# A searched table of leads sets every instruction's place in the scheduler's order; squares on ScalarE; the tail in two halves

## The chip, the core and the metric

The kernel runs on one core of a Trainium2 chip. A core has five engines that run their own instruction streams side by side: TensorE (PE in the profile; PEld is its weight load), VectorE (DVE), ScalarE (ACT), GpSimd (POOL) and SyncE (SP, which here issues the transfers). The metric is the device time of one execution in microseconds (us).

## The reference

A two-layer encoder over 512 tokens of width 1024, in float32. Cut to what is computed:

```
for l in range(2):
    z = rms_norm(x, g_mix) @ w_in            # q, k, v, recurrent input, gate
    o = rms_norm(diff_attention(rope(q), rope(k), v))      # 4 heads, two softmaxes each
    c = centred_dwconv(xb)
    r = rms_norm((rg_lru(c, forward) + rg_lru(c, backward)) * gelu(gb))
    x = x + concat(o, r) @ w_out
    x = x + cross_attention(rms_norm(x), rms_norm(mem))    # 4 heads, 256 tokens
    x = x + square(relu(rms_norm(x) @ w1)) @ w2            # 4096 wide
return rms_norm(x, g_final)
```

## The kernel before, in words

Activations lie feature-major: x is eight tiles `c_x0` to `c_x7` of 128 features by 512 tokens. A float32 product is made from two reduced-precision parts: each operand is split into a high part (a copy on ScalarE) and a low part (a subtraction on VectorE), and TensorE adds three products (high by high, high by low, low by high). A weight tile of 128 by 1024 is loaded by SP into `wraw`, and split into `whi` (ScalarE) and `wlo` (VectorE); there are three buffers of each. PSUM has three banks `mm` and five `at`.

**Stages.** Per layer: the mixer (input projection, differential attention, conv, recurrence with sigmoid gates, GeLU, and as filler between the heads the keys and values of the memory), the output projection and cross-attention, and the MLP. The MLP works in four blocks of 1024 hidden features. In a block `mlp_pair` (L1180) makes two hidden tiles: product, times the broadcast rstd `rb` on VectorE, and relu squared, also on VectorE (`t = max(t, 0) * t`); `left_pair` builds sums and differences of them and splits these. `seven` (L1000) multiplies a pair of weight tiles with seven products of half-size (Strassen-like) instead of eight, and adds each product to x on VectorE; `right_pair` prepares the weights in `wraw`, `pt`, `whi`, `wlo`.

**The tail.** After the last block the squares of all eight x tiles are added on VectorE into one tile (`nrm.add`), TensorE sums them over the features by a product with a column of ones (each of these float32 products shows as two records), VectorE scales and GpSimd takes the power -1/2, TensorE spreads the result over the partitions by transposes against `c_ident` (tile `at`), ScalarE copies it to `rb`. VectorE multiplies six tiles (already scaled by g_final on ScalarE), GpSimd two, and SP writes the eight tiles of 256 KB.

**What sets the order.** The kernel records every operation in a plan (`Plan.record`, L226) with a key: the TensorE time recorded so far, less a lead given by the code (`plan.ahead`: 12 us for splits, 65 us for loads, 3 us for attention). `Plan.schedule` (L272) then plays a list scheduler: engine by engine it places the operation with the smallest key that can start first by a table of assumed durations; an operation that needs another activation table gets 25 us added to its key (`SWITCH`). The outcome is a fixed order for each engine's in-order stream, emitted from L414; so nearly every row of the profile shows L414, and rows are told apart by tile names. Each engine waits on semaphores for the operands and the buffers of its next instruction, and whatever stands behind a waiting instruction waits too.

Of the kernel before, what the change touches and what calls it, by code (L numbers as in the profile page):

```python
# [11 lines left out]
F32 = mybir.dt.float32  # L12
# [31 lines left out]
ORDER = ["XYPp1Rr2B3bNK", "XY1Pp2Rr3BbNK"]  # L44
FILL = [[8.6, 7.6, 8.6, 7.6, 10.8, 9.7, 11.9, 6.5, 11.9, 7.6, 8.6, 10.8, 7.6, 5.4, 5.4, 7.6],
        [10.8, 7.6, 8.6, 7.6, 8.6, 10.8, 6.5, 10.8, 10.8, 10.8, 7.6, 7.6, 9.7, 3.2, 1.1, 6.5]]
LAG = 2
POOL_OUT = (0, 1)
ATT_AHEAD = 3
SPLIT_AHEAD = 12.0  # L50
LOAD_AHEAD = 65.0


PC = {}
# [96 lines left out]
class Plan:  # L151
# [7 lines left out]
    TABLE = 1.283  # L159
    SWITCH = 25.0  # L160
    WAIT = 2.5
    SETS = {"Exp": ("exp",), "Tanh": ("exp", "sig", "gelu"), "Sigmoid": ("sig",), "Sqrt": ("sqrt",),
            "Gelu_apprx_tanh": ("gelu",), "Sin": ("sin",)}

# [30 lines left out]
    def cost(self, eng, m, a, k):  # L195
        out = a[0] if a else k["out"]
        n = 1
        for d in out.shape[1:]:
            n *= d
        if eng == "pe":  # L200
            if m == "transpose":
                return 0.109
            f32 = a[1].root.dtype == F32
            if n < 64:
                return 0.224
            return n * 0.00176 if f32 else max(0.114, n * 0.000456)
        if m == "dma_start":
            return 0.06
        if eng == "act":
            t = 0.093 + n * 0.000833  # L210
            t += 0.093 * sum(isinstance(k.get(x), _View) for x in ("scale", "bias", "accum_out"))
            return t
        if eng == "dve":
            if m == "tensor_reduce":
                n = 512
            if m == "tensor_scalar_mul":
                return 0.066 + n * 0.0007
            ap = m == "scalar_tensor_tensor" and isinstance(a[2], _View)
            return 0.067 + n * 0.00105 + 0.06 * ap
        if eng == "pool" and n <= 4:  # L220
            return 1.0
        if eng == "pool":
            return 0.1 + n * (0.0022 if m != "memset" else 0.001)
        return 0.06

    def record(self, eng, m, a, k):  # L226
# [18 lines left out]
        if m == "dma_start":  # L245
            v = out[0] if out else k["in_"]
            op.bytes = 4
            for d in v.shape:
                op.bytes *= d
        if m == "activation":  # L250
            op.table = self.SETS.get(str(a[2]).split(".")[-1])
        for v in allv:
# [18 lines left out]

    def schedule(self):  # L272
        ops = self.ops
        for op in ops:
            op.preds.discard(op)
            op.behind -= op.preds | {op}
            op.npred = len(op.preds) + len(op.behind)
            for p in op.preds:
                p.succ[op] = True
            for p in op.behind:  # L280
                p.succ[op] = False
# [34 lines left out]
        def look(e):  # L316
            best, smin, tries = [], 1e18, 0
            for key, idx in cand[e]:
                op = ops[idx]
                st = max(free_at[e], op.ready)  # L320
                ok = True
                need = {}
                for r in op.new:
                    if r.tag in slots:
                        need[r.tag] = need.get(r.tag, 0) + 1
                for tag, n in need.items():
                    fr = sorted(slots[tag])[:n]
                    st = max(st, fr[-1])
                    w, h = waiting[tag], head[tag]
                    while h < len(w) and w[h] in placed:  # L330
                        h += 1
                    head[tag] = h
                    if st >= 1e17:
                        ok = False
                    elif w[h] != idx and n + sum(i > w[h] for i in alive[tag]) > spare[tag]:
                        ok = False
                tries += 1
                if ok:
                    if op.table and table not in op.table:
                        key += self.SWITCH  # L340
                        st += self.WAIT if st > free_at[e] else 0.0
                    best.append((st, key, idx))
                    smin = min(smin, st)
                if tries >= 60 and best:
                    break
            if not best:
                return None
            lim = smin + self.LOOK
            return min(((k, i, s) for s, k, i in best if s <= lim))

        dirty = set(self.engines)
        while left:
# [8 lines left out]
            _, idx, st = choice[e]  # L361
            op = ops[idx]
            cand[e].remove((op.key, idx))
            dur = op.dur
# [52 lines left out]
def trunk(tc, ctx, xT, memT, pos, W, par, outT):  # L417
# [18 lines left out]
    def T():  # L436
        return plan.tile("b", [P, S], F32)
# [24 lines left out]
    def raw_weight(l, t, ahead=None):  # L462
# [8 lines left out]
                SP.dma_start(out=raw, in_=W[l * NT + t])  # L471
        return raw

    def weight(l, t):
        raw = pre.pop(t, None) if l == 0 else None
        first = raw is not None
        if raw is None:
# [43 lines left out]
    def pc(l, name, i):  # L521
        o = l * NPL + PC[name] + i
        return prm[:, o:o + 1]

    ident = C([P, P], F32, "ident")
    G.memset(ident, 0.0)
# [470 lines left out]
        out[3] = [(dh[:, i * P:(i + 1) * P], dh[:, 512 + i * P:512 + (i + 1) * P]) for i in range(4)]  # L997
        return out

    def seven(l, ta, tb, left, ca, cb, order=range(4)):  # L1000

        w = right_pair(l, ta, tb)
        X, Y, Z = MM(), AT(), AT()
# [15 lines left out]
        add(ca, LO, X, ALU.add)  # L1019
        prod(2, Z, True)  # L1020
        add(ca, LO, Z, ALU.add)
        prod(6, X, False)
        add(cb, LO, X, ALU.subtract)
        prod(5, Y, True)
# [155 lines left out]
    def mlp_pair(l, bk, p, xs, rb):  # L1180

        ts = []
        for i in (2 * p, 2 * p + 1):
            pm = MM()
            gemm_fm(l, T_W1 + 8 * bk + i, xs, pm)
            t = T()
            V.tensor_tensor(t, pm, rb, op=ALU.mult)
            V.scalar_tensor_tensor(t, t, 0.0, t, op0=ALU.max, op1=ALU.mult)
            ts.append(t)
        return left_pair(*ts)  # L1190

# [21 lines left out]
    for l in range(DEPTH):  # L1213
# [64 lines left out]
        def finish(hd, h):  # L1278
# [3 lines left out]
                cat[h] = hd.out()  # L1282
            later(1, out)

        for u in range(16):
            h, qc = divmod(u, 4)
            if qc == 0:
# [50 lines left out]
        for bk in range(4):  # L1338
# [2 lines left out]
                nrm = Norm()  # L1341
                xs = [None] * KD
            for m in range(0, 8, 2):
                seven(l, T_W2 + 8 * bk + m, T_W2 + 8 * bk + m + 1, hid, m, m + 1)
                for c in (m, m + 1) if bk == 3 else ():
                    if l + 1 < DEPTH:
                        xs[c] = prep_x(l + 1, "g_mix", c, nrm)
                    else:
                        nrm.add(x[c])
                        xs[c] = T()  # L1350
                        A.activation(xs[c], x[c], AF.Copy, scale=prm[:, P_FINAL + c:P_FINAL + c + 1])
# [4 lines left out]
    rt = nrm.rstd(D, 4)  # L1356
    bp = AT()
    bcast(rt, 4, bp)
    rb = plan.tile("rb", [P, S], F32)
    A.activation(rb, bp, AF.Copy)  # L1360
    for c in POOL_OUT + tuple(c for c in range(KD) if c not in POOL_OUT):
        o = T()
        if c in POOL_OUT:
            G.tensor_tensor(o, xs[c], rb, op=ALU.mult)
        else:
            V.tensor_tensor(o, xs[c], bp, op=ALU.mult)
        SP.dma_start(out=outT[c * P:(c + 1) * P, :], in_=o)

    order = plan.schedule()
    plan.emit(tc, order)  # L1370
# [73 lines left out]
```

## Time and profile before

| | us |
|---|---|
| median of 3 runs | 1506.97 (1505.68 to 1511.34) |
| the profiled execution's own time | 1508.43 |
| its span, first to last instruction | 1506.6 |
| TensorE busy in it | 1446.8 (96%) |
| VectorE busy | 1159.3 (77%) |
| ScalarE busy | 731.7 (49%) |
| GpSimd busy | 26.5 (2%) |
| mean granted TensorE clock | 0.984 of full |

The span is what the trace shows; the profiled execution took 1.8 us more than it, and 1.5 us more than the median. A stage is read from a table of windows: the length of a window less TensorE's busy time is what TensorE waited, and the granted clock tells whether it ran at 2.4 GHz (1.00) or 1.2 GHz (0.50). The mixers lie at 30 to 200 us and 760 to 950 us, the MLPs at 408 to 760 us and 1145 to 1491 us.

### The profile page before, as it was taken

The page shows a single profiled execution, that of the slowest core. Times are in us where ns is not written, and L with a number is a line of the kernel's source. Part 1 is how long each engine was busy: PE and PEld are TensorE (multiplying, and loading weights), DVE is VectorE, ACT ScalarE, POOL GpSimd, SP SyncE. Part 2 cuts the span into 40 slices and gives each one's busy share as a digit, 9 for nine tenths or more (in the row PEclk, how much of TensorE's full clock was granted, in tenths as well). Part 3 has the DMA queues.
Part 4 walks back from the last instruction along what each step waited for, and adds up shares of the span by engine and source line. Part 5 has one row for each costly group of instructions (what it writes and reads, how often), then busy time and mean ns, then how long its engine had stood idle before and what let it go on. Part 6 is the DMA issues. An engine that isn't in the chain of part 4 may idle for free.

```text
span 1506.6 us, 20763 instructions
## 1 busy us (share of the span) xinstructions
PE 1446.8 (96%) x8038; PEld 1239.1 (82%) x8038; DVE 1159.3 (77%) x1959; ACT 731.7 (49%) x1105; POOL 26.5 (2%) x46
## 2 busy tenths in 40 slices
PE   8978999999999999999999989999999999999996
PEld 6756888888888989898887768888888898988985
DVE  7888886555679797887958799855556887969695
ACT  6587765334434343433534887643443433434343
POOL 1000000000000000000000000000000000000000
PEclk9988999999999999999999999999999999999998
DMA  5332442321222222222224444432122223232321
GB/s 198 112 101 71 144 153 92 112 70 43 99 97 93 104 99 98 98 96 101 85 103 121 112 106 149 137 112 83 59 70 84 99 99 112 82 104 89 118 84 58
DMA packets 47666, 152.43 MB, mean 101 GB/s; under 512 B 6096, under 2 KB 6224, under 8 KB 47568
## 3 DMA queue, kind: packets, MB, share of 16 engines
q1 hardware_dynamic: 47424, 150.85, 30.2%
q8 instruction: 63, 1.03, 0.3%
q14 instruction: 35, 0.29, 0.1%
q10 hardware_dynamic: 144, 0.26, 0.1%
HBM read 136.41 MB, written 2.10 MB: 92 GB/s over the span
## 4 chain that ended last, share of the span: by engine, by line
PE 80%; DVE 11%; ACT 4%; issue 2%; DMA 1%; SPq 1%; POOL 0%; DVEq 0%; ACTq 0%; POOLq 0%
PE mm L414 63%; PE at L414 18%; DVE b L414 6%; DVE wlo L414 3%; ACT b L414 3%; DVE pt L414 1%; ACT L414 1%; SPq L414 1%; DMA b<-b 1%; DVE s L414 1%; ACT whi L414 0%; POOL s L414 0%; DVE c_x L414 0%; DMA wraw<-in_memT 0%; DMA c_x<-in_xT 0%
## 5 line engine op out<-in xcount | busy, mean ns | idle before, releaser
L414 PE MATMUL mm<-b,whi 128*128 128x512 f32 (+1 forms) x3648 | 985.5, 358 | 11.7 <-ACT b L414 5.0
L414 PEld LDWEIGHTS mm<-b,whi 128*128 128x128 f32 x3648 | 638.5, 189 | 119.7 <-ACT b L414 6.3
L414 PE MATMUL mm<-b,wlo 128*128 128x512 f32 (+1 forms) x1824 | 650.1, 356 | 10.2 <-DVE wlo L414 10.2
L414 ACT ACTIVATE whi<-wraw 128x1024 fp32r<-128x1024 f32 (+1 forms) x223 | 233.4, 1048 | 357.4 <-issue 155.2
L414 PEld LDWEIGHTS mm<-b,wlo 128*128 128x128 f32 x1824 | 344.5, 189 | 67.4 <-DVE wlo L414 12.6
L414 DVE TENSOR_TENSOR wlo<-wraw,whi 128x1024 fp32r<-128x1024 f32 (+1 forms) x223 | 268.9, 1206 | 40.9 <-ACT whi L414 40.4
L414 DVE TENSOR_TENSOR b<-b,b 128x512 fp32r<-128x512 f32 (+2 forms) x390 | 224.7, 593 | 16.0 <-ACT b L414 14.4
L414 ACT ACTIVATE b<-b 128x256 fp32r<-128x256 f32 (+2 forms) x224 | 130.3, 596 | 150.2 <-DVE b L414 146.7
L414 DVE TENSOR_TENSOR c_x<-c_x,mm 128x256 f32<-128x256 f32 (+1 forms) x160 | 73.7, 471 | 77.8 <-PE mm L414 76.4
L414 ACT ACTIVATE whi<-pt 128x1024 fp32r<-128x1024 f32 x64 | 67.9, 1061 | 101.8 <-PE mm L414 75.7
L414 PE MATMUL at<-b,whi 128*128 128x256 f32 x512 | 92.0, 278 | 0.0
L414 DVE TENSOR_TENSOR b<-mm,rb 128x512 f32<-128x512 f32 x72 | 49.4, 687 | 53.5 <-PE mm L414 53.4
L414 DVE TENSOR_TENSOR wlo<-pt,whi 128x1024 fp32r<-128x1024 f32 x64 | 78.1, 1220 | 0.6 <-ACT whi L414 0.3
L414 ACT ACTIVATE b<-at,s 128x512 f32<-128x512 f32 (+2 forms) x100 | 61.0, 617 | 34.8 <-DVE s L414 34.1
L414 PEld LDWEIGHTS at<-b,whi 128*128 128x128 f32 x512 | 77.7, 188 | 0.0
L414 PE MATMUL at<-b,b 128*128 128x256 f32 (+1 forms) x320 | 67.3, 341 | 5.8 <-DMA b<-b 3.7
L414 DVE TENSOR_REDUCE s<-at 128x1 f32<-128x512 f32 (+1 forms) x80 | 54.3, 686 | 24.0 <-PE at L414 24.0
L414 PE MATMUL at<-b,wlo 128*128 128x256 f32 x256 | 71.2, 278 | 0.0
L414 PEld LDWEIGHTS at<-b,b 128*128 128x128 f32 x320 | 48.2, 196 | 13.6 <-DMA b<-b 4.4
L414 PE MATMUL at<-pt,b 128*128 128x256 f32 (+1 forms) x288 | 51.3, 325 | 4.9 <-ACT pt L414 2.9
L414 DVE TENSOR_TENSOR c_x<-c_x,at 128x256 f32<-128x256 f32 x96 | 40.0, 417 | 18.4 <-PE at L414 17.8
L414 PEld LDWEIGHTS at<-pt,b 128*128 128x128 f32 x288 | 43.8, 192 | 11.5 <-ACT pt L414 3.2
(124 smaller groups left out, 1267.0 us busy)
## 6 DMA issues: line engine op xcount, KB each, us to landing
wraw<-in_W SPq DMA_DIRECT2D x249, 512.0 KB, 3.3
b<-b SPq DMA_DIRECT2D x96, 128.0 KB, 2.3
wraw<-in_memT SPq DMA_DIRECT2D x4, 512.0 KB, 4.3
out_T<-b SPq DMA_DIRECT2D x8, 256.0 KB, 2.6
c_x<-in_xT SPq DMA_DIRECT2D x7, 256.0 KB, 6.1
wraw<-in_W SPq DMA_DIRECT2D x6, 256.0 KB, 4.8
c_x<-in_xT ACTq DMA_DIRECT2D x1, 256.0 KB, 3.2
c_prm<-in_par SPq DMA_DIRECT2D x1, 89.0 KB, 3.0
```

Of the source, the lines that this page charges most:

```text
L414: getattr(self.engines[op.eng], m)(*a, **k)
```

## The change

1. **The order.** A table of 6003 characters gives every recorded operation a lead of its own, in steps of 0.5 us (`L` is 0, `u` is 20 us earlier, `#` is 20 us later), subtracted from its key before the scheduler runs. The scheduler also counts a DMA issue on SP as 0.43 us instead of 0.06 us, and a table switch delays its candidate only in the comparison, no longer in the planned start.
2. **The MLP.** Relu and the factor rb become one VectorE instruction, and the square goes to ScalarE. 64 instructions move from VectorE to ScalarE.
3. **The tail.** The last `seven` makes its products in another order (`early`), so that the left half of the tokens (LO, 256 columns) is complete before the right half (HI). The norm is then made half by half: the squares of x6 and x7 on ScalarE by halves, and TensorE adds them in its product with ones, with the sum of the first six tiles, instead of two VectorE additions. VectorE multiplies x, g_final and the rstd in one instruction, so that six scalings on ScalarE go. SP writes 16 tiles of 128 KB.

`DMA_T` is empty, so `weight_dma` is not called; `PRE` is 0.

```
+LEAD_STEPS = '#$%&()*+,-./0123456789:;<=>?@ABCDEFGHIJKLMNOPQRSTUVWXYZ[]^_`abcdefghijklmnopqrstu'
+LEADS = (
+    'uQbHM@uWAmHHHHHIIILLuu8F0F$uFGK:X#CQD81#@#C#J#J:AIA1P5QLGIIIN6QCUBVMJIG_VPEHHCOTCEMGdGNGFFULJ_FGFUai'
...
         if m == "dma_start":
-            return 0.06
+            return 0.9 if eng == "pool" else 0.43
...
     def schedule(self):
         ops = self.ops
+        assert len(ops) == len(LEADS)
+        for op, c in zip(ops, LEADS):
+            op.key -= LEAD_STEPS.index(c) / 2 - 20.0
...
+                    at = st
                     if op.table and table not in op.table:
                         key += self.SWITCH
-                        st += self.WAIT if st > free_at[e] else 0.0
-                    best.append((st, key, idx))
+                        st += self.WAIT if st > free_at[e] else self.HOLD
+                    best.append((st, key, idx, at))
...
-    def seven(l, ta, tb, left, ca, cb, order=range(4)):
+    def seven(l, ta, tb, left, ca, cb, order=range(4), early=False):
...
         add(ca, LO, Z, ALU.add)
+        if early:
+            prod(5, Y, True)
+            add(cb, HI, Y, ALU.add)
+            prod(6, X, False)
+            add(cb, LO, X, ALU.subtract)
+            prod(3, Y, False)
+            add(cb, LO, Y, ALU.add)
+            prod(7, X, False)
+            add(cb, HI, X, ALU.subtract)
+            add(ca, HI, X, ALU.add)
+            prod(4, Z, True)
+            add(ca, HI, Z, ALU.add)
+            return
...
-            V.tensor_tensor(t, pm, rb, op=ALU.mult)
-            V.scalar_tensor_tensor(t, t, 0.0, t, op0=ALU.max, op1=ALU.mult)
+            V.scalar_tensor_tensor(t, pm, 0.0, rb, op0=ALU.max, op1=ALU.mult)
+            A.activation(t, t, AF.Square)
...
+    outs = [T() for c in range(KD)]
+    for cs in (LO, HI):
+        st = AT()
+        sq = T()
+        for i in range(2):
+            A.activation(sq[:, i * HT:(i + 1) * HT], x[6 + i][:, cs], AF.Square)
+        for c in range(2):
+            with plan.group():
+                for i, q in enumerate((nrm.acc[:, cs], sq[:, :HT], sq[:, HT:])):
+                    PE.matmul(st[:, c:c + 1], q[:, c * P:(c + 1) * P], ones[:, 0:1], start=(i == 0), stop=(i == 2))
...
+        for c in POOL_OUT + tuple(c for c in range(KD) if c not in POOL_OUT):
+            o = outs[c][:, cs]
+            if c in POOL_OUT:
+                G.tensor_tensor(o, xs[c][:, cs], rb, op=ALU.mult)
+            else:
+                V.scalar_tensor_tensor(o, x[c][:, cs], gfin(c), bp[:, :HT], op0=ALU.mult, op1=ALU.mult)
+            SP.dma_start(out=outT[c * P:(c + 1) * P, cs], in_=o)
```

**Place 1: TensorE in the mixer of layer 0, at the gates of the recurrence.** Each gate is a group of three products into an `mm` bank (`b` the conv output's high and low parts, `whi_878`, `wlo_894` the gate weights) that ScalarE then reads for its sigmoid. Before, these gates follow each other:

```order
L414 MATMUL mm_1029<-b_810,whi_878 128x512
L414 MATMUL mm_1029<-b_818,whi_878 128x512
L414 MATMUL mm_1029<-b_810,wlo_894 128x512
L414 MATMUL mm_1050<-b_810,whi_878 128x512
L414 MATMUL mm_1050<-b_818,whi_878 128x512
L414 MATMUL mm_1050<-b_810,wlo_894 128x512
L414 MATMUL mm_1057<-b_872,whi_878 128x512
L414 MATMUL mm_1057<-b_884,whi_878 128x512
L414 MATMUL mm_1057<-b_872,wlo_894 128x512
```

Now (gate weights `whi_908`, `wlo_918`) a gate is followed by an input projection, `mm_1034` with the weights `whi_940`, `wlo_975`:

```order
L490 MATMUL mm_1024<-b_805,whi_908 128x512
L490 MATMUL mm_1024<-b_813,whi_908 128x512
L490 MATMUL mm_1024<-b_805,wlo_918 128x512
L490 MATMUL mm_1034<-b_103,whi_940 128x512
L490 MATMUL mm_1034<-b_120,whi_940 128x512
L490 MATMUL mm_1034<-b_103,wlo_975 128x512
L490 MATMUL mm_1034<-b_149,whi_940 128x512
L490 MATMUL mm_1034<-b_163,whi_940 128x512
L490 MATMUL mm_1034<-b_149,wlo_975 128x512
```

Fifteen products of `mm_1034` (nine more rows like the last six) stand between the gate `mm_1024` and the next one, and its other nine stand among the gates behind; before, the whole projection came after the last gate and a run of attention products.

**Place 2: TensorE at the first weights of the MLP's second product, layer 0, block 0.** `whi_4173` is the buffer that has to be read to its end before `whi_4306` can be written into the same place; `at_4302` are the products between. Before:

```order
L414 MATMUL at_4283<-b_4190,whi_4173 128x256
L414 MATMUL at_4283<-b_4195,whi_4173 128x256
L414 MATMUL at_4283<-b_4190,wlo_4185 128x256
L414 MATMUL at_4302<-b_3933,whi_4225 128x256
...
L414 MATMUL at_4302<-b_4213,wlo_4234 128x256
L414 MATMUL mm_4326<-b_3885,whi_4306 128x256 x2
L414 MATMUL mm_4326<-b_3885,wlo_4323 128x256
```

Now the same two weights are `whi_4170` and `whi_4299`, and an MLP product of the first kind (`mm_4250`) and two half-size products stand between them:

```order
L490 MATMUL at_4206<-b_4183,whi_4170 128x256
L490 MATMUL at_4206<-b_4195,whi_4170 128x256
L490 MATMUL at_4206<-b_4183,wlo_4178 128x256
L490 MATMUL mm_4250<-b_3560,whi_4140 128x512
...
L490 MATMUL mm_4211<-b_4204,wlo_4256 128x256
L490 MATMUL at_4334<-b_3909,whi_4299 128x256
L490 MATMUL at_4334<-b_3918,whi_4299 128x256
```

Between the last use of the old weight and the first of the new one there were 12 products of 256 columns; now there are 24 of 512 columns and 24 of 256.

**Place 3: the tail, on TensorE and on SP.** TensorE before, behind the last product (`c_ones` is the column of ones, `c_ident` the spreading):

```order
L414 MATMUL mm_13888<-b_13478,wlo_13942 128x256
L414 MATMUL mm_13888<-b_13577,whi_13925 128x256
L414 MATMUL mm_13888<-b_13589,whi_13925 128x256
L414 MATMUL mm_13888<-b_13577,wlo_13942 128x256
L414 MATMUL at_14054<-c_ones_77,b_13743 128x1 x4
L414 MATMUL at_14063<-c_ident_68,s_14061 128x128 x4
```

And now, `at_14039` for the left half and `at_14052` for the right one:

```order
L490 MATMUL at_13929<-b_13583,wlo_13974 128x256
L490 MATMUL at_14039<-c_ones_72,b_13746 128x1
L490 MATMUL at_14039<-c_ones_72,b_13972 128x1 x2
L490 MATMUL at_14039<-c_ones_72,b_13746 128x1
L490 MATMUL at_14039<-c_ones_72,b_13972 128x1 x2
L490 MATMUL at_14052<-c_ones_72,b_13746 128x1
L490 MATMUL at_14052<-c_ones_72,b_14047 128x1 x2
L490 MATMUL at_14052<-c_ones_72,b_13746 128x1
L490 MATMUL at_14052<-c_ones_72,b_14047 128x1 x2
L490 MATMUL at_14061<-c_ident_68,s_14056 128x128 x2
L490 MATMUL at_14080<-c_ident_68,s_14066 128x128 x2
```

The sums of both halves stand in front of the left half's spreading, all behind the last product. SP's writes, in the new order:

```order
L490 DMA out_T<-b_14070 128x256
L490 DMA out_T<-b_14072 128x256
L490 DMA out_T<-b_14075 128x256
L490 DMA out_T<-b_14077 128x256
L490 DMA out_T<-b_14083 128x256
L490 DMA out_T<-b_14087 128x256
```

Ten more such rows follow them; before, there were eight writes of 128x512.

## Rows read from the trace of the kernel before

**Rows 1.** The page: busy time of each engine, share of the span.

```profile
PE 1446.8 (96%) x8038; PEld 1239.1 (82%) x8038; DVE 1159.3 (77%) x1959; ACT 731.7 (49%) x1105; POOL 26.5 (2%) x46
```

**Rows 2.** Windows by stage: length, busy of each engine, granted clock, DMA share, GB/s.

```profile
30.00:200.00 170.00, 151.08 (x720) 122.89 (x719) 146.89 (x264) 125.45 (x204) 6.82 (x13) 0.92 0.37 106
408.00:760.00 352.00, 345.64 (x2152) 307.03 (x2152) 290.25 (x480) 138.63 (x177) 1.01 (x1) 1.00 0.28 98
600.00:610.00 10.00, 10.00 (x44) 8.06 (x43) 7.31 (x12) 3.36 (x5) 0.00 (x0) 1.00 0.22 72
760.00:950.00 190.00, 179.34 (x919) 148.61 (x918) 159.40 (x272) 128.38 (x205) 5.69 (x8) 0.97 0.39 118
1145.00:1491.00 346.00, 340.66 (x2129) 303.19 (x2128) 283.27 (x470) 137.39 (x175) 1.01 (x1) 1.00 0.26 91
1491.00:1507.00 16.00, 2.33 (x14) 1.68 (x12) 5.64 (x10) 1.84 (x3) 3.50 (x3) 0.63 0.35 131
```

**Rows 3.** Windows over the stretches at half the granted clock, ahead of the tail.

```profile
95.70:105.90 10.20, 6.63 (x16) 4.78 (x15) 10.20 (x13) 8.96 (x13) 0.00 (x0) 0.50 0.37 116
112.80:126.40 13.60, 8.20 (x26) 6.43 (x26) 9.85 (x21) 13.44 (x24) 1.01 (x1) 0.50 0.09 33
191.30:194.60 3.30, 3.15 (x15) 3.16 (x16) 3.30 (x9) 2.10 (x5) 0.00 (x0) 0.50 0.41 150
839.80:846.60 6.80, 6.29 (x18) 5.13 (x19) 3.03 (x6) 5.61 (x8) 0.00 (x0) 0.50 0.60 133
870.60:873.90 3.30, 3.30 (x9) 2.56 (x9) 3.30 (x5) 2.25 (x5) 0.00 (x0) 0.50 0.00 0
```

**Rows 4.** Timeline of TensorE, 93 to 121 us: start, length, what, [idle before <-releaser].

```profile
99.86 1.22 PE L414 MATMUL mm<-b,whi 128*128 128x512 f32 x2 [3.56 <-ACT b L414]
...
120.68 0.58 PE L414 MATMUL at<-c_ones,b 128*128 128x1 f32 x2 [5.09 <-ACT b L414]
```

**Rows 5.** Timeline of ScalarE, 93 to 100 us.

```profile
93.74 0.58 ACT L414 ACTIVATE pt<-at 128x512 fp32r<-128x512 f32 x1
94.32 1.28 ACT L414 ACT_TABLE_LOAD   x1
95.62 2.19 ACT L414 ACTIVATE b<-b 128x512 f32<-128x512 f32 x4
```

**Rows 6.** Timeline of all engines, 470 to 474 us.

```profile
471.04 1.07 ACT L414 ACTIVATE whi<-wraw 128x1024 fp32r<-128x1024 f32 x1 [0.58 <-PE at L414]
...
472.38 1.22 DVE L414 TENSOR_TENSOR wlo<-wraw,whi 128x1024 fp32r<-128x1024 f32 x1
...
473.65 0.38 PE L414 MATMUL mm<-b,wlo 128*128 128x256 f32 x1 [1.00 <-DVE wlo L414]
```

**Rows 7.** Groups of instructions: count, busy us, mean ns, idle before and its releaser.

```profile
L414 DVE SCALAR_TENSOR_TENSOR b<-b 128x512 f32<-128x512 f32 x64 | 44.1, 689 | 1.4
L414 ACT ACTIVATE b<-c_x 128x512 f32<-128x512 f32 x56 | 34.4, 618 | 9.1 <-DVE c_x L414 7.6 <-DMA c_x<-in_xT 1.5
L414 DVE SCALAR_TENSOR_TENSOR b<-mm,rb 128x512 f32<-128x512 f32 x16 | 11.1, 691 | 31.5 <-PE mm L414 31.5
L414 DVE SCALAR_TENSOR_TENSOR b<-wraw,c_prm,b 128x256 fp32r<-128x256 f32 x16 | 7.2, 476 | 0.0
```

**Rows 8.** Timeline of all engines, 1491 us to the end.

```profile
1491.20 0.42 DVE L414 TENSOR_TENSOR c_x<-c_x,mm 128x256 f32<-128x256 f32 x1 [1.78 <-PE mm L414]
...
1493.79 1.05 PE L414 MATMUL at<-c_ones,b 128*128 128x1 f32 x8 [2.63 <-DVE b L414]
...
1496.25 1.11 PE L414 MATMUL at<-c_ident,s 128*128 128x128 f32 x4 [1.41 <-POOL s L414]
1497.40 0.60 ACT L414 ACTIVATE rb<-at 128x512 f32<-128x512 f32 x1 [4.50 <-PE at L414]
...
1498.75 4.48 SPq L414 DMA_DIRECT2D out_T<-b  x8
```

**Rows 9.** Timeline of SP, 48 to 54 us: back-to-back issues of 128 KB.

```profile
48.68 4.96 SPq L414 DMA_DIRECT2D b<-b  x8
```

More of the change, by code (lines that the diff above doesn't have):

```diff
@@ L46 @@
         [10.8, 7.6, 8.6, 7.6, 8.6, 10.8, 6.5, 10.8, 10.8, 10.8, 7.6, 7.6, 9.7, 3.2, 1.1, 6.5]]
+PRE = [0.0, 0.0]
 LAG = 2
@@ L161 @@
     WAIT = 2.5
+    HOLD = 0.0
     SETS = {"Exp": ("exp",), "Tanh": ("exp", "sig", "gelu"), "Sigmoid": ("sig",), "Sqrt": ("sqrt",),
@@ L249, in record @@
                 op.bytes *= d
+            if "accum_op" in k:
+                op.bytes *= 2
         if m == "activation":
@@ L348, in look @@
             lim = smin + self.LOOK
-            return min(((k, i, s) for s, k, i in best if s <= lim))
+            return min(((k, i, s, at) for s, k, i, at in best if s <= lim))
         dirty = set(self.engines)
@@ L360, in schedule @@
             e = pick[1]
-            _, idx, st = choice[e]
+            _, idx, _, st = choice[e]
             op = ops[idx]
@@ L472, in raw_weight, with weight_dma @@
         return raw
+    def weight_dma(l, t):
+        hi = plan.tile("whi", [P, 1024], F32R)
+        lo = plan.tile("wlo", [P, 1024], F32R)
+        src = W[l * NT + t]
+        with plan.ahead(CAST_AHEAD):
+            G.dma_start(out=hi, in_=src)
+        with plan.ahead(NEG_AHEAD):
+            A.activation(lo, b(hi), AF.Copy, scale=-1.0)
+            G.dma_start(out=lo, in_=src, accum_op=ALU.add)
+        return hi, lo
     def weight(l, t):
+        if t in DMA_T:
+            return weight_dma(l, t)
         raw = pre.pop(t, None) if l == 0 else None
@@ L523, in pc, with gfin @@
         return prm[:, o:o + 1]
+    def gfin(c):
+        return prm[:, P_FINAL + c:P_FINAL + c + 1]
     ident = C([P, P], F32, "ident")
@@ L1283, in finish @@
             later(1, out)
+        fill(PRE[l])
         for u in range(16):
@@ L1343, in trunk @@
             for m in range(0, 8, 2):
-                seven(l, T_W2 + 8 * bk + m, T_W2 + 8 * bk + m + 1, hid, m, m + 1)
+                end = l + 1 == DEPTH and bk == 3
+                seven(l, T_W2 + 8 * bk + m, T_W2 + 8 * bk + m + 1, hid, m, m + 1, early=end and m == 6)
                 for c in (m, m + 1) if bk == 3 else ():
-                    if l + 1 < DEPTH:
+                    if not end:
                         xs[c] = prep_x(l + 1, "g_mix", c, nrm)
-                    else:
+                    elif m < 6:
                         nrm.add(x[c])
+                    if end and c in POOL_OUT:
                         xs[c] = T()
-                        A.activation(xs[c], x[c], AF.Copy, scale=prm[:, P_FINAL + c:P_FINAL + c + 1])
+                        A.activation(xs[c], x[c], AF.Copy, scale=gfin(c))
             if bk < 3:
@@ L1354, in trunk @@
             hid = nxt
[L1356 to L1367, printed above, removed]
+    outs = [T() for c in range(KD)]
[8 more added lines that the diff above has]
+                    PE.matmul(st[:, c:c + 1], q[:, c * P:(c + 1) * P], ones[:, 0:1], start=(i == 0), stop=(i == 2))
+        ms = SM(2)
+        V.tensor_scalar(ms, st[:, :2], 1.0 / D, EPS, op0=ALU.mult, op1=ALU.add)
+        rt = rsqrt_small(ms, 2)
+        bp = AT()
+        bcast(rt, 2, bp)
+        rb = plan.tile("rb", [P, HT], F32)
+        A.activation(rb, bp[:, :HT], AF.Copy)
+        for c in POOL_OUT + tuple(c for c in range(KD) if c not in POOL_OUT):
[5 more added lines that the diff above has]
+            SP.dma_start(out=outT[c * P:(c + 1) * P, cs], in_=o)
     order = plan.schedule()
```

63 lines of the change are left out of this document (added).

## The prediction

> **What bounds the kernel now.** I read the page first. TensorE is busy for 96% of the span, VectorE for 77%, ScalarE for 49% [rows 1]. So the time is TensorE's work plus what TensorE waits for or does slowly, and a change of order, which takes no product away, can only win that part back. The second view is the table of windows by stage, and there the reader is to subtract TensorE's busy time from the length. The mixers lose 170 - 151.08 = 18.9 us (layer 0) and 190 - 179.34 = 10.7 us (layer 1); the MLPs lose 352 - 345.64 = 6.4 us and 346 - 340.66 = 5.3 us; from the last product to the end nearly nothing but the tail runs, 13.7 us without TensorE [rows 2]. Cross-attention, between these windows, loses nothing.
>
> The third view is the granted clock. Five stretches ahead of the tail have 0.50, which is 1.2 GHz in place of 2.4 [rows 3]. What TensorE did in them would have taken half as long. Layer 0: (6.63 + 8.20 + 3.15) / 2 = 9.0 us; layer 1: (6.29 + 3.30) / 2 = 4.8 us. The two longest stretches lie at and behind the two longest waits of the mixer, 3.56 us that ended at 99.86 and 5.09 us that ended at 120.68 [rows 3, 4]: the engine stood still, then ran slow. Where such a wait goes, I expect the slow stretch to go with it.
>
> So the most that can be won ahead of the tail is 27.9 us (mixer 0) + 15.5 (mixer 1) + 11.7 (both MLPs) = 55 us. Less is to be had in mixer 0, because VectorE is busy there for 146.89 us of the 170 [rows 2]: with unchanged VectorE work that stage cannot get shorter than that, a gain of at most 23.1 us.
>
> **Mixer, layer 0: -12 us.** The wait of 3.56 us was for ScalarE to read a gate's bank. ScalarE had a table load, four square roots and another load in front of the sigmoids: 1.28 + 2.19 us and again a load [rows 5]. The new order puts fifteen products of the input projection between two gates there (place 1). In a stretch of the MLP without a gap, 44 products of 512 columns fill 10 us, 0.23 us each [rows 2] (a single record is longer, since neighbours overlap); fifteen last 15 x 0.23 = 3.5 us, which is the wait's length. The wait of 5.09 us was that of a head's norm for a square on ScalarE [rows 4]; that norm now stands behind two and a half projections more. These two waits, with half of the work in the slow stretches behind them, (6.63 + 8.20) / 2 = 7.4 us, are 16.1 us. The ends are 23.1 us (VectorE never idle) and a loss of 5 us (one new wait as long as the worst one now). I take 12: VectorE would then be busy for 147 of 158 us, 93%, and I do not expect more from an in-order engine whose operands come from two others. What is late next is VectorE itself.
>
> **Mixer, layer 1: -7 us.** Here VectorE (159 of 190 us) leaves room, and ScalarE (128) too [rows 2], so the end is all 15.5 us; the other end is a loss of 3 us, the two table loads that the new ScalarE order has more (34 instead of 32, both in this stage), 2 x 1.28 = 2.6 us [rows 5], if each holds TensorE up. I take somewhat under half of the 15.5: the moves are of the same kind as in layer 0, but the waits are short and many.
>
> The extra loads are where a rule of the Trainium skill speaks against the new order. The load in front of the square roots took 1.28 us, started when the instruction before it ended (93.74 + 0.58 = 94.32) and was followed at 95.62 by the next activation: 1.3 us for the whole switch [rows 5]. The Trainium skill (ScalarE: Activation LUTs, Table sets: the hidden batching unit) asks to batch calls by set, and its section on what a load costs puts a switch at 2.66 us with a drain. By that the two would cost 5.3 us of ScalarE time, an estimate from that page, and this case's trace does not show the second half of it.
>
> **MLP, both layers: -9 us.** Two things happen. VectorE loses 64 instructions of 689 ns, 44.1 us [rows 7], and keeps the others at the same price: the product with rb was a two-operand instruction and is now one that also takes the maximum, which the trace has at 691 ns on the same operands [rows 7]. That is 22 us less in each MLP's 290 us [rows 2]. ScalarE gets 64 squares of 618 ns [rows 7], 20 us in each MLP where it is busy for 139 of 352 us [rows 2]; they are hidden as long as ScalarE stays under half, and no table load comes with them, since the squares of the norm run between other functions without one. Each hidden tile crosses one engine more, some 0.1 us of handover, in front of sums that are not due for a block.
>
> The second thing is the order at the weights. TensorE's waits of the MLP are of one kind: ScalarE may write the new `whi` only when TensorE is done with the old one (start 471.04, 1.07 us), VectorE then writes `wlo` (472.38, 1.22 us), and TensorE starts at 473.65 after a wait of 1.00 us [rows 6]. The chain from release to use is 2.6 us; the 12 products between last about 1.6 us. In the new order 24 products of 512 and 24 of 256 columns stand there (place 2), more than 8 us. So this wait goes by order alone, and where the order leaves a short distance the freed VectorE shortens the chain only by its queueing. Ends: 11.7 us (all waits) and 2 us (the two waits of 1.6 to 1.7 us, for x on VectorE, shortened a little). I take 9, nearer to the upper end, since both causes pull the same way.
>
> **Tail: +2 us.** This part I expect to lose. Count from the end of the last product, 1491.2 [rows 8]; the span ends at 1506.6, 15.4 us later. What goes: the square and two additions on VectorE, so that the sums start at once instead of at +2.6. What comes: eight records of the sums took 1.05 us [rows 8]; with three terms for each of four columns there are 24, some 3.1 us, and both halves stand in front of the first spreading (place 3), so that it starts at about +3.1. Two of the four transposes take 0.55 us, the copy of half a row 0.4 (the full one is 0.60) [rows 8], and VectorE's first multiplication 0.48 us (nearest row: 476 ns for 256 columns with a column operand [rows 7]): the first write can be issued at about +4.7, instead of at 1498.75 = +7.55 [rows 8]. That is 2.9 us gained. But there are 16 writes. Back to back SP issued eight transfers of 128 KB in 4.96 us, 0.62 us each [rows 9]; 16 take 9.9 us, to +14.6. Before, the eight issues ended at 1498.75 + 4.48 = +12.0, and the span 3.4 us later [rows 8]; with smaller last transfers I take 2.8 us: +17.4, so 2 us later than now. Ends: -2.9 us, if issuing hid behind the data, and +3.5.
>
> The Trainium skill (DMA: Bandwidth & Descriptors, Issuing engines are not separate DMA queues) calls the sequencer's time to start a transfer usually small beside the transfer. By that the 16 issues would be hidden and the tail would give 2.9 us instead of costing 2. The row of SP disagrees for this size: 0.62 us of issue each [rows 9], and there are 16.
>
> **The sum.** -12 - 7 - 9 + 2 = -26 us on a span of 1506.6, so 1480.6; the profiled execution took 1.8 us more than its span, and 1508.43 - 26 = 1482.4. The median of the runs is 1.5 us below that execution: 1481 us. All lower ends give 1506.97 - 23.1 - 15.5 - 11.7 - 2.9 = 1454, all upper ones 1506.97 + 5 + 3 - 2 + 3.5 = 1516.
>
> **Rivals.**
> *The stalls only move* (14 in 100). In the mixers VectorE and ScalarE are busy for 74 to 86% of the time, so an order planned on assumed durations may exchange one wait for another. Against it: the waits are few and long, and place 1 puts ready work exactly there. Mixers 0, MLP -9, tail +2: 1500 us.
> *The stalls nearly all go* (20 in 100). For it: cross-attention shows that TensorE can run 200 us without a gap, and without waits the clock has no reason to fall. Mixer 0 at VectorE's floor -23, mixer 1 -13, MLP -11, tail +1: 1461 us.
> *Slower* (6 in 100). The projection of place 1 moves ahead by some 12 us, and with it the moment at which its weights must be split, 1.07 us on ScalarE and 1.22 on VectorE [rows 6], on engines that were full there (10.20 of 10.20 and 8.96 of 10.20 us [rows 3]). If a split comes late, all of TensorE's queue stands behind the projection's product. Each mixer has five or more projections moved that way: 3 us of lateness at five of them in each layer is 30 us, with mean gain elsewhere of 9 and a tail of +2 that is 1507 + 30 - 7 = 1530 us. It decides from a lateness of about 1.5 us each, where it makes 15 us and the sum is +8.
> *The tail does as its halves suggest*, by hidden issues: inside the forecast, 1476 us.
>
> **How the numbers follow.** The forecast case has 60 in 100, with a range of its own of 1468 to 1494. 0.5% (7.5 us) is about what a measurement of this kernel can tell from no change: faster is below 1499.4, slower above 1514.5. Faster: 60 + 20 + about a third of the second case = 85; same: the rest of that case, 9; slower 6. From 1462 to 1500 I leave out most of the slower case, part of the case of moved stalls and the lower half of the best one.
>
> **What would show it.** Right: in the window of mixer 0 no slow stretch of 10 us, and at most 7 us of TensorE's idle time; the MLP windows with under 3 us of waits for `wlo` and x, and VectorE 22 us less busy in each; in the tail the first write 4 to 5 us after the last product, 16 issues of about 0.6 us, and an end more than 16 us behind the last product. Wrong: waits of several us for `wlo` of a projection in the mixers, the half clock as long as now, or a tail under 14 us.

## The result and the profile after

The changed kernel took 1470.24 us (median of 4 runs, 1465.47 to 1471.38) against 1507.05 us: a ratio of 0.9741, 95% interval 0.9722 to 0.9759. In a second set of runs it was 0.9736 (0.9723 to 0.9749). That is 37 us less; the forecast was 1481 us, 26 less, with a range of 1462 to 1500. The profiled execution took 1471.38 us, its span 1469.6, 37.0 less than before.

The page, the line of the engines; it answers to [rows 1]:

```profile
PE 1436.2 (98%) x8054; PEld 1232.6 (84%) x8054; DVE 1116.2 (76%) x1901; ACT 762.3 (52%) x1168; POOL 28.1 (2%) x49
```

VectorE lost 43.1 us of work and ScalarE got 30.6 (squares in, six scalings out). TensorE is 10.6 us less busy, with the same products and 16 short records more in the tail. The windows say why; the columns are those of [rows 2]:

```profile
30.00:186.00 156.00, 147.46 (x716) 119.24 (x715) 143.44 (x264) 123.92 (x203) 6.84 (x12) 0.98 0.41 115
168.00:175.00 7.00, 6.66 (x30) 6.07 (x31) 5.72 (x16) 3.00 (x8) 2.39 (x2) 0.51 0.46 112
...
393.60:740.40 346.80, 345.64 (x2153) 308.12 (x2151) 270.87 (x447) 154.90 (x209) 1.01 (x1) 1.00 0.29 99
740.40:924.00 183.60, 176.14 (x917) 146.56 (x916) 156.60 (x269) 130.82 (x207) 5.63 (x8) 0.98 0.41 121
826.80:830.30 3.50, 3.05 (x10) 2.50 (x10) 1.29 (x4) 2.87 (x7) 0.00 (x0) 0.51 0.14 54
878.00:881.50 3.50, 3.50 (x11) 2.92 (x12) 3.50 (x6) 1.32 (x4) 0.00 (x0) 0.51 0.76 188
1119.00:1455.60 336.60, 336.25 (x2132) 300.18 (x2130) 264.48 (x439) 150.85 (x203) 1.01 (x1) 1.00 0.28 93
1455.60:1469.60 14.00, 3.57 (x29) 2.91 (x27) 5.62 (x15) 1.49 (x4) 4.18 (x6) 0.60 0.45 150
```

The edges are those of the same TensorE record, counted from the start, as in the windows of before. A new order puts a few other products between two edges, so lengths alone mislead a little; the safer measure is what TensorE loses: its idle time, and half of what it did at 0.50.

| stage | lost before, us | lost after, us | change | forecast |
|---|---|---|---|---|
| mixer, layer 0 | 18.9 + 9.0 = 27.9 | 8.5 + 6.66/2 = 11.8 | -16.1 | -12 |
| mixer, layer 1 | 10.7 + 4.8 = 15.5 | 7.5 + (3.05 + 3.50)/2 = 10.7 | -4.8 | -7 |
| MLPs | 6.4 + 5.3 = 11.7 | 1.2 + 0.4 = 1.5 | -10.2 | -9 |
| last product to the end (length) | 15.4 | 14.0 | -1.4 | +2 |

These make -32.5 of the 37.0. The rest, some 4.5 us, is TensorE's own busy time at full clock, nearly all in the MLP of layer 1 (340.66 to 336.25 us for as many records). Its products of 512 columns follow each other every 0.233 us before and after; those of 256 columns follow every 0.113 or 0.118 us, in stretches, and in this window more often at the shorter step than before. Part of that is chance: the same order of this MLP took 338.35 us in another execution (the whole writes below). The rest of its cause stays open.

Each row of the table is one execution before and one after. How far the rows of the mixers can be trusted, the traces of all kernels below tell, counted in the same way: without the table's order mixer 0 loses 26.0 to 29.5 us and mixer 1 13.3 to 15.5 (five traces), with it 10.0 to 11.8 and 7.4 to 11.4 (eight traces).

In the timeline of TensorE at place 1, the two waits of [rows 4] are gone. Between 88 and 130 us these four are the only waits of over 0.2 us:

```profile
92.06 0.73 PE L490 MATMUL mm<-b,whi 128*128 128x512 f32 x2 [0.45 <-DVE b L490]
93.25 0.73 PE L490 MATMUL mm<-b,whi 128*128 128x512 f32 x2 [0.23 <-ACT b L490]
104.68 0.47 PE L490 MATMUL at<-b,b 128*128 128x512 f32 x1 [1.35 <-DMA b<-b]
129.30 0.62 PE L490 MATMUL at<-c_ident,s 128*128 128x128 f32 x4 [0.71 <-DVE s L490]
```

The longest slow stretch that is left, 168.1 to 174.9 us, has no long wait ahead of it. TensorE waited 0.56, 0.81 and 0.30 us there, and the stretch began in these products of one column:

```profile
167.49 3.07 PE L490 MATMUL at<-c_ones,b 128*128 128x1 f32 x16 [0.30 <-ACT b L490]
```

The tail, which answers to [rows 8], from the end of the last product at 1455.6:

```profile
1455.45 2.74 PE L490 MATMUL at<-c_ones,b 128*128 128x1 f32 x24
...
1458.05 0.43 PE L490 MATMUL at<-c_ident,s 128*128 128x128 f32 x2
...
1458.52 0.38 ACT L490 ACTIVATE rb<-at 128x256 f32<-128x256 f32 x1 [1.69 <-PE at L490]
1458.94 2.83 DVE L490 SCALAR_TENSOR_TENSOR b<-c_x,c_prm,at 128x256 f32<-128x256 f32 x7 [0.55 <-ACT rb L490]
...
1459.45 7.72 SPq L490 DMA_DIRECT2D out_T<-b  x16
```

The first write is issued 3.85 us after the last product, and the 16 issues take 0.48 us each.

### The profile page after: what moved, and what is told of

The parts are those of the page before. It is cut to its first block, busy times and chain, and to the rows that moved or that the text cites. A ratio compares the mean times of both kernels' runs of the same rounds, so it can differ in the third digit from the quotient of the medians.

```text
span 1469.6 us, 20813 instructions
## 1 busy us (share of the span) xinstructions
PE 1436.2 (98%) x8054; PEld 1232.6 (84%) x8054; DVE 1116.2 (76%) x1901; ACT 762.3 (52%) x1168; POOL 28.1 (2%) x49
## 4 chain that ended last, share of the span: by engine, by line
PE 83%; DVE 10%; ACT 3%; DMA 1%; issue 1%; SPq 0%; POOL 0%; DVEq 0%; ACTq 0%
PE mm L490 63%; PE at L490 19%; DVE b L490 7%; ACT b L490 2%; DVE wlo L490 1%; DVE s L490 1%; DMA b<-b 1%; ACT whi L490 1%; ACT L490 1%; DVE pt L490 1%; SPq L490 0%; POOL s L490 0%; DMA wraw<-in_W 0%; DMA c_x<-in_xT 0%; ACT pt L490 0%
## 5 line engine op out<-in xcount | busy, mean ns | idle before, releaser
L490 DVE TENSOR_TENSOR b<-b,b 128x512 fp32r<-128x512 f32 (+3 forms) x388 | 222.4, 593 | 10.0 <-ACT b L490 8.5
L490 ACT ACTIVATE b<-b 128x512 fp32r<-128x512 f32 (+2 forms) x288 | 168.7, 602 | 78.8 <-DVE b L490 76.7
L490 DVE SCALAR_TENSOR_TENSOR b<-mm,rb 128x512 f32<-128x512 f32 x80 | 55.1, 689 | 108.1 <-PE mm L490 107.7
L490 PE MATMUL at<-b,pt 128*128 128x256 f32 x384 | 55.4, 278 | 0.0
L490 PEld LDWEIGHTS at<-b,pt 128*128 128x128 f32 x384 | 49.6, 188 | 0.4
```

The source lines that it names most:

```text
L490: getattr(self.engines[op.eng], m)(*a, **k)
```

## The experiments

Each ran beside the kernel before on the same chip; ratios are to that kernel.

**The squares alone** (before, with the MLP's two lines):

```
-            V.tensor_tensor(t, pm, rb, op=ALU.mult)
-            V.scalar_tensor_tensor(t, t, 0.0, t, op0=ALU.max, op1=ALU.mult)
+            V.scalar_tensor_tensor(t, pm, 0.0, rb, op0=ALU.max, op1=ALU.mult)
+            A.activation(t, t, AF.Square)
```

> The kernel before with one edit: relu and rb in one VectorE instruction, the square on ScalarE; no table, old tail. Theory A (the order of the table made the gain; the freed VectorE alone doesn't shorten the chain PE release, whi, wlo, use): VectorE loses about 44 us of busy time, but TensorE's waits of the MLPs (11.7 us before) fall by 1 to 3 us only; 1504 to 1506 us, ratio 0.997 to 0.999. Theory B (the freed VectorE makes the MLP gain of about 14 us that the trace after shows): 1492 to 1495 us, ratio 0.990 to 0.992.

Measured: 0.9995 (0.9986 to 1.0004), no change. Its windows of the two MLPs:

```profile
405.80:757.80 352.00, 345.43 (x2153) 306.75 (x2152) 274.27 (x449) 155.88 (x209) 1.01 (x1) 1.00 0.29 98
1142.30:1488.40 346.10, 340.37 (x2129) 302.82 (x2127) 267.14 (x438) 154.67 (x207) 1.01 (x1) 1.00 0.28 91
```

VectorE has 16 us less to do in each, and TensorE waits as long as before (6.6 and 5.7 us). The timeline at the first weights of the second product, the place of [rows 6]:

```profile
468.71 1.06 ACT L414 ACTIVATE whi<-wraw 128x1024 fp32r<-128x1024 f32 x1 [0.59 <-PE at L414]
...
469.69 0.69 DVE L414 TENSOR_TENSOR pt<-pt,wraw 128x512 f32<-128x512 f32 x1
470.30 1.22 DVE L414 TENSOR_TENSOR wlo<-wraw,whi 128x1024 fp32r<-128x1024 f32 x1
...
471.57 0.39 PE L414 MATMUL mm<-b,wlo 128*128 128x256 f32 x1 [1.20 <-DVE wlo L414]
```

The free time lies elsewhere: at this place VectorE has a `pt` in front of `wlo`, and TensorE gets there too soon.

**The tail alone** (before, with the `early` order of the last `seven`, the norm by halves and the 16 writes, as in the diff above):

> The kernel before with the new tail alone (last seven in the early order, norm by halves, 16 writes of 128 KB). The prediction's step said +2 us: 1509. The trace after shows 14.0 us from the last product to the end in place of 15.4 and 0.48 us an issue in place of 0.62, so theory A now: -1 to -2 us, 1505 to 1506, with SP's issues at 0.45 to 0.50 us each. Rival: without the table the halves are not kept apart on VectorE and TensorE and the tail takes 15 to 18 us, 1507 to 1510.

Measured: 0.9995 (0.9986 to 1.0005). Its tail is shorter in the trace, 14.4 us, with 7.71 us for 16 issues; one us is less than these runs can tell. The forecast's +2 is refuted in the trace, a gain of the whole is not shown.

**Everything but the table**:

```
-        for op, c in zip(ops, LEADS):
+        for op, c in zip(ops, 'L' * len(LEADS)):
```

> The kernel after with every lead at 0: all edits of the code and of the scheduler's costs stay, only the table is gone. Theory A (the table makes nearly all): mixers lose as much as before (layer 0 about 19 us idle and 25 us at half clock), ratio to before 0.993 to 1.005, 1497 to 1514 us. Theory B (squares and costs make at least half): ratio 0.983 to 0.988, 1481 to 1489 us.

Measured: 1.0001 (0.9992 to 1.0011). Squares, tail and the scheduler's new costs together give nothing that shows. In the windows the mixer of layer 0 waits 21.2 us (18.9 before), and the MLPs wait as before, 6.4 and 5.0 us:

```profile
30.40:201.30 170.90, 149.71 (x720) 121.17 (x719) 145.74 (x263) 123.89 (x205) 6.45 (x13) 0.94 0.37 104
...
408.90:761.30 352.40, 346.01 (x2153) 307.32 (x2153) 274.31 (x448) 155.86 (x209) 1.01 (x1) 1.00 0.30 98
...
1145.80:1491.00 345.20, 340.17 (x2132) 302.83 (x2130) 267.60 (x440) 151.71 (x203) 1.01 (x1) 1.00 0.28 91
```

No run has the table with the scheduler's old costs, so what the new costs are worth beside the table is not shown.

**The table with the old squares** (the first experiment's edit, backwards, in the kernel after):

> The kernel after with the table, but with relu and square on VectorE as before (each pair of instructions keeps its two places and leads). Theory A: MLPs keep most of their gain by order, VectorE some 44 us more busy; 1470 to 1476 us, ratio to before 0.976 to 0.980. Theory B (the table only works with the freed VectorE): MLP waits come back in full or more, 1484 to 1492 us, ratio 0.985 to 0.990.

Measured: 0.9887 (0.9871 to 0.9903). Theory A had expected that the order alone keeps the MLPs' gain, and it is wrong. The mixers keep theirs (10.0 and 11.3 us lost, by the measure of the table above) and so does the tail (14.0 us); the MLPs lose all of it. Windows of the MLPs, 6.8 and 5.4 us of idle time, and in the second a slow stretch besides (clock 0.99):

```profile
391.80:745.70 353.90, 347.10 (x2153) 306.73 (x2152) 288.71 (x479) 137.48 (x177) 1.01 (x1) 1.00 0.29 97
1124.80:1473.10 348.30, 342.92 (x2131) 304.43 (x2130) 283.47 (x471) 133.50 (x171) 1.01 (x1) 0.99 0.27 90
```

The waits are not where they were. At place 2 (first row) TensorE has no wait any more; it waits elsewhere in the same MLP:

```profile
457.05 0.48 PE L490 MATMUL at<-b,whi 128*128 128x256 f32 x2
...
542.29 0.38 PE L490 MATMUL mm<-b,wlo 128*128 128x256 f32 x1 [1.00 <-DVE wlo L490]
...
641.42 1.65 PE L490 MATMUL at<-b,pt 128*128 128x256 f32 x12 [1.50 <-DVE c_x L490]
```

So in the MLPs the squares are worth nothing without the table and the table nothing without the squares. Whether VectorE's time is the reason, or a table made for other instructions, the next run tells.

**The same order, VectorE's relu made twice**:

```
-            for m, a, k in op.calls:
+            for m, a, k in op.calls * (2 if twice else 1):
```

`twice` holds for the 64 relu instructions of the MLPs.

> The kernel after, in the very same order, but VectorE makes each of the 64 relu-times-rb instructions of the MLPs twice (the same operands and result), 64 x 689 ns = 44 us more VectorE work, as much as the squares had; ScalarE keeps the squares. Theory A (the table's order of the MLPs needs the VectorE time): MLP waits return, 14 to 24 us in all, 1484 to 1494 us, ratio 0.985 to 0.991. Theory B (the table with the old squares lost its MLP gain because its leads were made for other instructions): the repeated work is hidden, 1470 to 1474 us, ratio 0.975 to 0.979.

Measured: 0.9873 (0.9847 to 0.9898). The MLPs' waits are back, 7.1 and 7.6 us, in an order that has not changed, so it is VectorE's time that this order needs:

```profile
391.80:747.20 355.40, 348.31 (x2152) 308.72 (x2152) 290.75 (x479) 157.33 (x209) 1.01 (x1) 0.99 0.29 97
1122.60:1471.10 348.50, 340.91 (x2132) 303.00 (x2130) 284.76 (x471) 152.33 (x203) 1.01 (x1) 1.00 0.27 90
```

The timelines of VectorE show how, first in the kernel after, where TensorE has no wait here:

```profile
526.53 0.68 DVE L490 TENSOR_TENSOR pt<-pt,wraw 128x512 f32<-128x512 f32 x1
527.14 0.68 DVE L490 SCALAR_TENSOR_TENSOR b<-mm,rb 128x512 f32<-128x512 f32 x1
527.74 1.22 DVE L490 TENSOR_TENSOR wlo<-wraw,whi 128x1024 fp32r<-128x1024 f32 x1
```

and with the relu twice, followed by TensorE's row:

```profile
526.62 0.69 DVE L493 TENSOR_TENSOR pt<-pt,wraw 128x512 f32<-128x512 f32 x1
527.22 1.41 DVE L493 SCALAR_TENSOR_TENSOR b<-mm,rb 128x512 f32<-128x512 f32 x2
528.55 1.22 DVE L493 TENSOR_TENSOR wlo<-wraw,whi 128x1024 fp32r<-128x1024 f32 x1
...
529.82 0.38 PE L493 MATMUL at<-b,wlo 128*128 128x256 f32 x1 [1.20 <-DVE wlo L493]
```

VectorE has no gap in either. In the kernel after, `wlo` was done at 528.96, and TensorE came to it 0.7 us later:

```profile
529.64 0.28 PE L490 MATMUL at<-b,wlo 128*128 128x256 f32 x1
```

With the relu twice TensorE came at 528.62 and `wlo` was done at 529.77: VectorE had fallen behind TensorE by more than the order's distance. A VectorE that is busy for 78% on average is full for microseconds at a time, and what stands in front of a weight there is paid by TensorE.

**The table for the mixers only, and for the MLPs only** (`'L'` for the operations of the MLPs, and for those of the mixers and cross-attention):

> The kernel after with the leads of both MLPs at 0; mixers, cross-attention and tail keep theirs, squares stay on ScalarE. Theory A (the order gains by stage, and the MLP gains only with both, table and freed VectorE): mixers lose 11 to 13 us each as in the kernel after, MLPs wait 11 to 12 us again, 1484 to 1487 us, ratio to before 0.985 to 0.987. Rival (freed VectorE suffices once the mixers hand over early): MLP waits under 4 us, 1471 to 1476 us, 0.976 to 0.980.

> The complement: leads at 0 in the mixers and cross-attention, the table's own in both MLPs and the tail. Theory A: mixers lose 28 and 15 us as before, MLPs under 3 us of waits, tail 14 us: 1490 to 1494 us, ratio 0.989 to 0.992. Rival (the MLP order rests on what the mixer before it left in the buffers): MLP waits of 6 us or more stay, 1498 us or more, 0.994 and up.

Measured: 0.9822 (0.9805 to 0.9839) and 0.9902 (0.9885 to 0.9919). The two gains, 1.78% and 0.98%, add to 2.76%, with the tail counted twice; the whole is 2.6%. The first ratio lies below theory A's range (0.985 to 0.987) and above its rival's, but the MLPs' waits, 6.0 and 5.0 us, are theory A's; the second ratio lies in theory A's range. Windows of the mixer of layer 0 and of the MLP behind it, for the mixers' table:

```profile
28.40:184.10 155.70, 148.12 (x720) 119.88 (x719) 144.37 (x270) 124.25 (x204) 6.24 (x12) 0.98 0.41 115
391.70:743.20 351.50, 345.51 (x2152) 307.33 (x2151) 274.36 (x449) 156.77 (x211) 1.01 (x1) 1.00 0.29 98
```

and for the MLPs' table:

```profile
29.90:201.90 172.00, 152.99 (x719) 123.56 (x718) 146.18 (x263) 124.08 (x205) 6.45 (x13) 0.92 0.37 104
409.60:754.50 344.90, 343.37 (x2152) 305.70 (x2151) 271.28 (x448) 154.44 (x209) 1.90 (x1) 1.00 0.30 100
```

The MLP of the last row waits 1.5 us, and that of layer 1 0.5. Each stage loses its waits whatever the order of the others: the stalls did not move on.

**Three late weights**, for the price of a wait (the kernel after; three ScalarE copies to `whi` in the MLP of layer 0 repeated 8, 12 and 18 times):

```
+LATE = {1969: 8, 2317: 12, 2665: 18}
-            for m, a, k in op.calls:
+            for m, a, k in op.calls * LATE.get(op.idx, 1):
```

> The kernel after, in the same order, with three copies of weights (whi) in the MLP of layer 0 made 8, 12 and 18 times over on ScalarE, so that they end 7.5, 11.8 and 18.2 us later; TensorE has no wait over 1.2 us in that stage otherwise. Theory A (a long wait is followed by the half clock, which costs again): after the waits of about 5, 9 and 15 us the granted clock is 0.50 for 3 to 14 us each, and a stretch at 0.50 doubles the step of a product of 512 columns from 0.23 to about 0.46 us. Rival (the clock falls by chance, not by waits): full clock after all three, and the MLP is longer by the waits alone.

Measured: 1509.05 us, in a single execution. The waits, in TensorE's timeline:

```profile
482.30 0.80 PE L492 MATMUL mm<-b,whi 128*128 128x256 f32 x2 [5.83 <-ACT whi L492]
...
580.54 0.80 PE L492 MATMUL at<-b,whi 128*128 128x256 f32 x2 [10.10 <-ACT whi L492]
...
682.20 0.80 PE L492 MATMUL mm<-b,whi 128*128 128x256 f32 x2 [16.00 <-ACT whi L492]
```

The windows over the three stretches at 0.50, the only ones of that stage:

```profile
480.40:487.20 6.80, 4.43 (x19) 4.14 (x20) 3.69 (x6) 2.87 (x3) 0.00 (x0) 0.50 0.12 41
572.50:586.20 13.70, 5.20 (x22) 4.90 (x23) 3.89 (x5) 8.72 (x9) 0.00 (x0) 0.50 0.11 37
668.10:688.60 20.50, 5.85 (x24) 5.27 (x25) 6.42 (x12) 15.25 (x15) 0.00 (x0) 0.50 0.09 26
```

Every one of these waits brought the half clock, in a stage that has none in the kernel before and in the kernel after. It began during the wait and ended 4.9, 5.6 and 6.4 us behind it; TensorE was busy in it for 4.43, 5.20 and 5.85 us, so the clock cost 2.2, 2.6 and 2.9 us on top of 5.8, 10.1 and 16.0: far from in proportion to the wait. Together that is 39.6 us, and the run was 38.8 us longer than the kernel after. Theory A holds, but its upper sizes were too large.

Waits of about 2 us are not so sure. In the mixer of layer 1 a wait for a transfer, 1.80 us up to 826.20 in the kernel after, was followed by the slow stretch at 826.8; in the kernel with two queues, further down, the same wait was longer, and the clock stayed at 1.00:

```profile
823.88 0.70 PE L490 MATMUL at<-b,b 128*128 128x512 f32 x2 [2.10 <-DMA b<-b]
...
815.00:835.00 20.00, 17.39 (x88) 13.98 (x86) 14.91 (x27) 17.74 (x29) 0.00 (x0) 1.00 0.43 106
```

**Two ways to end sooner**, beside the kernel after itself:

> The kernel after itself, as the measure for the two kernels beside it: ratio to before 0.972 to 0.977, tail of 14.0 us from the last product to the end.

```
-            SP.dma_start(out=outT[c * P:(c + 1) * P, cs], in_=o)
+            (A if cs is HI and c in (2, 3, 4, 7) else SP).dma_start(out=outT[c * P:(c + 1) * P, cs], in_=o)
```

> The kernel after, in which four of the right half's eight writes are issued by ScalarE, the other twelve by SP. Theory A (SP's 16 issues of 0.48 us set the end of the tail, 7.7 of its 14 us): SP needs 12 x 0.48 = 5.8 us, then the last product of VectorE sets the end; the tail takes 11.5 to 12.5 us, the whole 1.5 to 2.5 us less, 0.9983 to 0.9990 of the kernel after. Rival (the landings set the end, issue is hidden): tail 13.5 to 14.2 us, no difference.

```
-            SP.dma_start(out=outT[c * P:(c + 1) * P, cs], in_=o)
+            if cs is HI:
+                SP.dma_start(out=outT[c * P:(c + 1) * P, :], in_=outs[c])
```

> The kernel after with the halves computed as now, but with eight writes of 256 KB, each issued when both halves of its tile are there (8 operations of the left half go, the leads of the rest stay). The prediction's step (16 issues cost more than the halves win): the tail gets 1.5 to 3 us shorter, 11 to 12.5 us. Theory A now (an early start of the left half's writes pays for the issues): the first write is issued some 2.5 us later, eight issues of about 0.55 us and 3.4 us to the last landing make a tail of 14 to 15.5 us, 0 to 1.5 us longer.

Measured: 0.9736 (0.9723 to 0.9749) for the kernel after, 0.9718 (0.9701 to 0.9735) with two queues, 0.9720 (0.9707 to 0.9733) with whole writes. The intervals overlap, so neither is shown to be faster. In the traces, one of each, their tails are 12.9 and 13.25 us against 13.95; the eight traces with the tail of the kernel after lie between 13.94 and 14.23. With two queues SP issues twelve writes and ScalarE four, side by side:

```profile
1455.22 5.90 SPq L490 DMA_DIRECT2D out_T<-b  x12
...
1457.68 2.93 ACTq L490 DMA_DIRECT2D out_T<-b  x4
```

With whole writes SP begins 5.4 us after the last product, 1.5 us later than in the kernel after, and needs 4.48 us instead of 7.72:

```profile
1457.74 4.48 SPq L491 DMA_DIRECT2D out_T<-b  x8
```

So in these traces SP's issues are not hidden in the tail, and fewer of them make it shorter; the whole writes' 13.25 us lie between what the two theories expected, the two queues' 12.9 between theory A (11.5 to 12.5) and its rival.

## Why the prediction was right, and where its steps were not

**The bound.** TensorE's waits and its slow clock were nearly all that there was to win: 32.5 of the 37 us came from the four stages named. The 4.5 us of shorter busy time lie outside the bound ("can only win that part back"); no step had them. The stalls did not move, and the late weights of place 1 did not come (the timeline there shows no wait for `whi` or `wlo`; the whole mixer has 0.6 and 0.8 us of them, elsewhere). "The stalls nearly all go" came true in the MLPs, not in the mixers, where 16.0 us of waits are left. The 1470 us lie about halfway between the forecast of 1481 and that rival's 1461. The 11 us beyond the forecast are 4.1 of mixer 0, 1.2 of the MLPs, 3.4 of the tail and the 4.5, less 2.2 of mixer 1. The time lies inside the range, then, with a size missed in nearly every step, most of them to the same side. A reading under the first rival was wrong: ScalarE is busy for 68% of mixer 1 (128.38 of 190 us, [rows 2]), not 74 or more.

**Mixer 0: -12 forecast, -16.1 measured.** The mechanism held: both long waits went and took their slow stretches with them, and nothing but the table does it. The two waits with their slow stretches were sized at 16.1 us, and as much went; the discount from 16 to 12 for a full VectorE was the mistake. That the two agree to 0.1 us is luck: idle time fell by 10.4 us and the slow clock's cost by 5.7, where the sum had 8.65 and 7.4, since smaller waits went too and the slow stretch at 168 us came. VectorE was busy for 143.44 of 156 us, 92%, as forecast. That was no limit to the waits: the window got 14 us shorter, and the new order has about 3 us more of products in it. "At most 7 us of idle time" was missed with 8.5.

**That the slow clock goes with the wait** was an assumption from two places. The late weights show it for waits of 5.8 us and more. Below that it holds only in part: a wait of 2.10 us brought none, and the stretch at 168 us came without a wait of over 0.81. Its price was put at 3.3 and 4.1 us for the two; 2.2 to 2.9 us was measured for each single wait; the stretches of the mixer held smaller waits as well.

**Mixer 1: -7 forecast, -4.8 measured.** Mis-sized. Of the 7.5 us of waits that remain, 3.2 end with VectorE, 3.0 with transfers, 1.0 with GpSimd and 0.2 with ScalarE. The two more table loads came (34 of 1283 ns in the trace); no run separates them, but hardly a wait of TensorE ends with ScalarE. The Trainium skill (ScalarE: Activation LUTs, What ACT_TABLE_LOAD costs) puts a switch at 2.66 us with a drain, by which the two would put 5.3 us on ScalarE, an estimate from that page. The traces before and after show no drain: behind every load but the first of a kernel the next activation starts 0.01 us after the load's end.

**MLPs: -9 forecast, -10.2 measured.** The size was right and the reason wrong. The freed VectorE time was 16 us in each MLP with the squares alone and 19 in the kernel after (290.25 to 270.87 and 283.27 to 264.48), not 22: 64 rows of 689 ns were added up, and neighbouring rows overlap (527.14 and 527.74 above start 0.60 us apart, and the first lasts 0.68). 32 times 0.60 is the 19; why the squares alone free only 16 is not shown. The step said that the wait at place 2 "goes by order alone" and that the two causes pull the same way. At place 2 itself that holds: no wait is left there with the table and the old squares, 0.32 us with the relu twice. The mistake was to let place 2 stand for the whole MLP. With the order alone as much waiting stands at other places (0.9887, all of its gain outside the MLPs), and free VectorE time alone gives nothing (0.9995): the order's distances hold everywhere only when VectorE is not packed in front of `wlo` and x. The two do not add; they need each other.

**Tail: +2 forecast, -1.4 measured.** Three terms were mis-sized. The first write came at +3.85, not +4.7: the sums of 24 records took 2.74 us, not 3.1, and the spreading started at +2.45. The 16 issues took 7.72 us, not 9.9: the rate of 0.62 us was that of transfers between tiles [rows 9], while the eight output writes of before had 4.48 / 8 = 0.56 [rows 8]. The last landing and the end took 2.4 us, not 2.8. Together 3.4 us, and the sign "more than 16 us behind the last product" failed with 14.0. That 16 issues in a row cost something was right, fewer make the traced tail shorter; that they cost more than the halves win was wrong. The Trainium skill (DMA: Bandwidth & Descriptors, Issuing engines are not separate DMA queues) calls the time to start a transfer usually small beside the transfer. Hidden issues would have given -2.9 us by the prediction's sum; the trace's -1.4 lies between that and +2.

## What to carry to other kernels

An instruction taken off a busy in-order engine can be worth nothing until the order uses the time, and a better order can be worth nothing until the engine has it: measure the two together and apart before dropping either. One wait that goes does not show that its stage is cured; count the waits of the whole stage. A wait of TensorE of 6 to 16 us cost here its length and two to three us more at half clock; a wait of about 2 us brought the half clock in some executions only. For the price of an issue take the row of the same kind of transfer.

## What the runs showed that was not expected

The half clock behind a wait hardly grew with it: 4.9 us behind 5.8 us of waiting, 6.4 behind 16. And TensorE's time at full clock moved, with no wait to explain it: in the MLP of layer 1, 336.25 us after against 340.66 before; 339.87 with the table for the mixers only, 339.85 with that for the MLPs only, and 338.35 with the kernel after's order and whole writes. Part of it is the execution's chance, then; what the order has to do with it is open.
